# Down projection and second norm of a decoder layer: places of raw operands, order of their loads and splits, order of the norms' steps

## Chip, cores and metric

The kernel is one program on one core of one Trainium2 chip. The metric is the device time of one execution in microseconds (us). The engines named below are PE (TensorE, matrix products), DVE (VectorE), ACT (ScalarE), POOL (GpSimd) and SP (SyncE, whose queue issues most DMAs). PSUM is the memory in which PE accumulates; the kernel's PSUM tiles of 128 x 512 floats are called banks here.

## What is computed

One decoder layer in float32 on 1024 tokens of width 1024: two attention mixers, a gated merge, a norm, a SwiGLU feed-forward network of width 2816, and a second norm. The part that matters here is the last:

```python
def layer_norm(x, g, b):
    mu = jnp.mean(x, axis=-1, keepdims=True)
    xc = x - mu
    var = jnp.mean(xc * xc, axis=-1, keepdims=True)
    return xc * lax.rsqrt(var + LN_EPS) * g + b

def swiglu(u, w_gate_up, w_down):
    hg, hu = jnp.split(u @ w_gate_up, 2, axis=-1)
    return (silu(hg) * hu) @ w_down

y = mixer(x * (1.0 + scale_m) + shift_m, ...)
x = layer_norm(ALPHA * x + (1.0 + gate_m) * y, ln1_g, ln1_b)
y = swiglu(x * (1.0 + scale_f) + shift_f, ...)
x = layer_norm(ALPHA * x + (1.0 + gate_f) * y, ln2_g, ln2_b)
```

## The kernel before

**Two-term floats.** A float32 operand is held as two fp32r tiles, a rounded high part and the rest. `split` (L168) makes them: ACT copies the operand into the high tile (L169), then DVE subtracts that from the operand into the low tile (L170). A product of two operands is three matmuls (high x high, high x low, low x high; L1706).

**Seven products.** The down projection h (1024 tokens x 2816) times w_down (2816 x 1024) is done by Strassen's scheme in the Winograd form: seven products of half-size blocks in place of eight, over sums and differences of blocks. `ORDER` (L1521) gives their order, (0, 1, 2, 3, 5, 4, 6); the text counts them first to seventh as they are run. Each product has 11 units (NP), so the units are numbered u = 0 to 76. Unit u brings 128 rows of each operand, one tile from h and one from w_down, together 128 x 1024 floats, and makes 12 matmuls: four blocks of tokens (t), three terms each.

The sums of blocks (names `hs_d` and `wt2_d` in the code; the trace calls the second `wt_d`) are made earlier, during the up projection and the first products, by three "lanes" of `sum_set`, each with tiles of its own: it fetches four tiles, subtracts and adds on DVE, and writes four tiles to DRAM. `sums_ahead` (L1574) starts a lane's next set when the step p of the up projection is below a limit of that lane. The very last set, ("h", 10), is fetched on POOL's queue and not on ACT's.

**Loads and splits.** `dn_load` fetches a unit's two tiles on SP's queue (L1595, L1597) into a raw place: tiles `r1` and `r2` in two buffers each, so four places in turn. `dn_prepare` splits units up to a given one and, after each split, loads up to `ahead` = 4 units more. The split goes to an operand place (`dn_place`): eight tiles of pool `bigu`, six of `low`, two made of the small tiles `w_hi` and `w_lo` (these units are split in two halves of 512), and from unit 33 on one more, `a_raw` and `a_lo`. In the product loop `dn_prepare` stands at the start of unit u and runs 12, then 14, then 15 units ahead of PE.

**Banks and adds.** There are two sets of four banks. `bank_a` is used by the first, third, sixth and seventh product, `bank` by the second, and then again by the fourth and fifth. Three products start from zero (first, second, fourth in this order); every other one accumulates on top of what its banks hold, since in this scheme the results are running sums. After each product `dn_add` reads the banks: it multiplies by the gate (L1700) and adds to the tile `z` of the residual (L1701). The first matmul of the next product on that bank comes behind this read. The last three units of the fourth and fifth product (`shared`) are done block by block, so that a block is finished, and added, before the next one starts; the others before the seventh finish their four blocks in the last unit. The seventh is done block by block altogether: all 11 units for t = 0, then for t = 1, and so on.

**Norms.** `gain` (L1372, L1373) multiplies half a row block of `z` by the first norm's scale and adds its shift; there are 16 such pairs, placed by the table `GAINS` at (product, unit). `half_stats` (L1268) takes the moments of half a row block. `norm_shared` is a generator with three parts: moments and square root (L1273 to L1276); reciprocal, a small product and ACT's scaling of the row block (L1295 to L1297); scale, shift and the store (L1299 to L1301). `norm_steps` moves every norm in the list `norms` one part on. In the seventh product three rounds of `norm_steps` stand ahead of each block's add, and a fourth after it. The last block goes through `norm_quick`.

Instructions stand in program order on each engine (`manual_schedule`), so a `split` or a `gain` that stands ahead of a `dn_add` on DVE is done ahead of it.

## Time and profile before

| what | value |
|---|---|
| time, median of 3 runs | 1798.02 us (1797.59 to 1798.94) |
| the profiled execution's own time | 1797.99 us |
| span of its trace | 1796.2 us |
| PE busy | 1762.3 us, 98% |
| DVE busy | 1197.9 us, 67% |
| ACT busy | 846.0 us, 47% |
| POOL busy | 504.9 us, 28% |
| down projection, first to last matmul | 1554.03 to 1782.47 us |

The shares are means over the whole span, over stages with different limits; a single stage is read from the timeline and from the busy time in windows. In a timeline a row gives start, length, engine, line, operation, output<-inputs, tile shapes and a count of like instructions; in brackets stands the idle time ahead of it and who ended that. "Granted clock" is the share of its full speed that PE ran at. In a list of waits a row gives who waited for whom, the time in us, how many times, and the longest. `dn` names raw tiles and split operands alike, `pf` and `px` are banks, `zt` is the residual `z`, `g` the product of bank and gate.

### The profile page before, as it was taken

To read this page: it belongs to the slowest core of one execution; us is meant where nothing else is said; L and a number is where in the kernel's file an instruction comes from. 1 tells how busy PE (TensorE), PEld (TensorE's weight loads), DVE (VectorE), ACT (ScalarE), POOL (GpSimd) and SP (SyncE) were. 2 spreads that over 40 slices of the span, in tenths; PEclk is the share of its full clock that TensorE was granted. 3 is DMA by queue.
4 is the path that set the end of the run, shared out by engine and by line. 5 is a ranking of instruction groups with operands and counts; after the bars stand their busy time and mean duration, and the time that the engine had idled before them with its cause. 6 is when DMAs were issued, how large, how long until landed. Compare 5 with 4: busy or idle time off the path is not lost.

```text
span 1796.2 us, 24740 instructions
## 1 busy us (share of the span) xinstructions
PE 1762.3 (98%) x8774; PEld 1448.2 (81%) x8774; DVE 1197.9 (67%) x2141; ACT 846.0 (47%) x1739; POOL 504.9 (28%) x338
## 2 busy tenths in 40 slices
PE   9999999999999999999999999999999999999796
PEld 7888888888888888788888888888888888888585
DVE  7655566567566766658656865766666666578967
ACT  6554454544444677764441224743434333444431
POOL 0232233233233332125204753143334334100000
PEclk9999999999999999999999999999999999999898
DMA  9222323333332332266576442146656665587741
GB/s 363 84 69 80 104 78 91 109 90 94 97 89 83 85 101 72 71 241 226 174 239 222 162 132 100 36 164 226 229 214 244 212 245 189 196 273 234 244 143 71
DMA packets 130844, 277.30 MB, mean 154 GB/s; under 512 B 19296, under 2 KB 29088, under 8 KB 130720
## 3 DMA queue, kind: packets, MB, share of 16 engines
q1 hardware_dynamic: 116544, 246.80, 41.3%
q10 hardware_dynamic: 13392, 26.29, 4.4%
q0 software_dynamic: 784, 2.63, 0.4%
q8 instruction: 69, 1.13, 0.2%
q14 instruction: 55, 0.45, 0.1%
HBM read 203.99 MB, written 58.03 MB: 146 GB/s over the span
## 4 chain that ended last, share of the span: by engine, by line
PE 84%; DVE 10%; ACT 2%; DMA 2%; issue 1%; SPq 0%; DVEq 0%; ACTq 0%
PE pf L1037 21%; PE pj L191 9%; PE pj L193 9%; PE pj L192 9%; PE p L1037 6%; PE s L623 4%; PE p L191 3%; PE p L193 3%; PE p L192 3%; PE po L684 3%; PE pt L661 3%; PE pf L1706 2%; DVE dn L170 2%; DVE g L1700 1%; DVE zt L1701 1%
## 5 line engine op out<-in xcount | busy, mean ns | idle before, releaser
L191 PE MATMUL pj<-u,w_hi 128*128 128x512 f32 x736 | 302.7, 411 | 0.0
L193 PE MATMUL pj<-u,w_lo 128*128 128x512 f32 x736 | 288.8, 392 | 0.0
L192 PE MATMUL pj<-u,w_hi 128*128 128x512 f32 x736 | 288.2, 392 | 0.0
L550 POOL TENSOR_TENSOR rb<-rb,sin_t 128x512 f32<-128x512 f32 x64 | 85.7, 1339 | 518.2 <-DVE rb L548 483.4
L145 DVE TENSOR_TENSOR w_lo<-r,w_hi 128x512 fp32r<-128x512 f32 x128 | 122.7, 964 | 102.3 <-ACT w_hi L144 94.9
L79 DVE TENSOR_TENSOR w_lo<-w_raw,w_hi 128x512 fp32r<-128x512 f32 x132 | 122.9, 934 | 82.0 <-ACT w_hi L78 81.5
L191 PEld LDWEIGHTS pj<-u,w_hi 128*128 128x128 f32 x736 | 138.6, 188 | 31.6 <-issue 6.2
L1706 PE MATMUL pf<-dn 128*128 128x512 f32 x630 | 151.9, 395 | 11.5 <-DVE g L1700 11.5
L193 PEld LDWEIGHTS pj<-u,w_lo 128*128 128x128 f32 x736 | 138.3, 188 | 30.6
L639 ACT ACTIVATE probs<-probs,st 128x128 f32<-128x128 f32 (+1 forms) x320 | 145.6, 461 | 31.0 <-DVE st L628 30.7
L192 PEld LDWEIGHTS pj<-u,w_hi 128*128 128x128 f32 x736 | 138.9, 189 | 22.2
L1706 PEld LDWEIGHTS pf<-dn 128*128 128x128 f32 x630 | 119.6, 190 | 37.9 <-ACT dn L169 9.6
L78 ACT ACTIVATE w_hi<-w_raw 128x512 fp32r<-128x512 f32 x132 | 81.8, 622 | 93.1 <-PE p L192 55.0
L551 POOL TENSOR_TENSOR r<-ra,rb 128x512 f32<-128x512 f32 x63 | 116.1, 1843 | 4.9
L663 ACT ACTIVATE ptsb<-pt 128x512 f32<-128x512 f32 (+1 forms) x128 | 63.5, 548 | 101.5 <-PE pt L661 101.2
L169 ACT ACTIVATE dn<-dn 128x1024 fp32r<-128x1024 f32 x66 | 69.6, 1059 | 84.6 <-DMA dn<-wt_d 35.1
L170 DVE TENSOR_TENSOR dn<-dn 128x1024 fp32r<-128x1024 f32 x66 | 79.1, 1221 | 40.2 <-ACT dn L169 40.0
L564 ACT ACTIVATE qs<-r 64x1024 fp32r<-64x1024 f32 x38 | 40.2, 1058 | 100.1 <-POOL r L551 99.6
L144 ACT ACTIVATE w_hi<-r 128x512 fp32r<-128x512 f32 x128 | 79.4, 622 | 12.5 <-DVE gate L1499 4.9
L126 POOL TENSOR_TENSOR s<-r 128x512 f32<-128x512 f32 x27 | 35.8, 1327 | 174.9 <-DVE w_lo L145 92.1
L565 DVE TENSOR_TENSOR qs<-r,qs 64x1024 fp32r<-64x1024 f32 x38 | 46.4, 1220 | 57.2 <-ACT qs L564 56.5
L623 PE MATMUL s<-kh,qs 128*128 128x256 f32 (+1 forms) x320 | 79.7, 283 | 1.8 <-DVE st L628 1.7
(447 smaller groups left out, 4321.5 us busy)
## 6 DMA issues: line engine op xcount, KB each, us to landing
w_raw<-in_w_in SPq DMA_DIRECT2D x100, 256.0 KB
r<-in_w_gate_up SPq DMA_DIRECT2D x44, 512.0 KB
a_raw<-in_w_ada SPq DMA_DIRECT2D x24, 512.0 KB
dn<-hs_d SPq DMA_DIRECT2D x44, 256.0 KB
dn<-wt_d SPq DMA_DIRECT2D x44, 256.0 KB
h_d<-g SPq DMA_DIRECT2D x39, 256.0 KB
dn<-h_d SPq DMA_DIRECT2D x33, 256.0 KB
dn<-in_w_down SPq DMA_DIRECT2D x33, 256.0 KB
```

Of the source, the lines that this page charges most:

```text
L79: self.nc.vector.tensor_tensor(lo, raw, hi, op=OP.subtract)
L145: self.nc.vector.tensor_tensor(lo, src, hi, op=OP.subtract)
L170: nc.vector.tensor_tensor(lo, src, hi, op=OP.subtract)
L191: nc.tensor.matmul(ps, w[0], m[0], start=first, stop=False)
L192: nc.tensor.matmul(ps, w[0], m[1], start=False, stop=False)
L193: nc.tensor.matmul(ps, w[1], m[0], start=False, stop=last)
L550: eng.tensor_tensor(b, b, sin_t[:, s], op=OP.mult)
L551: eng.tensor_tensor(residue_half(res, r, t), by_residue(a, r), by_residue(b, r), op=OP.add)
L623: nc.tensor.matmul(pss[h][:, i, lo:], box["q"][h][:, b * P:(b + 1) * P], ks[h][:, (b - 1 + lo) * P:(b + 1) * P], start=i == 0 and n == 0, ...
L639: nc.scalar.activation(pr, pr, AF.Exp, scale=-1.0, bias=st[:, 0, h, b:b + 1], accum_out=st[:, 1, h, b:b + 1])
L1037: nc.tensor.matmul(ps, w[:, c], m[:, k], start=first and k == 0 and n == 0, stop=k == 3 and n == 2, skip_group_check=True)
L1706: nc.tensor.matmul(ps, op[x][0][:, c], op[y][1], start=first and n == 0, stop=last and n == 2, skip_group_check=True)
```

## The change

**Raw places.** A function `raw_place` gives them now. Units 0 to 11 use the same four. From unit 12 on the two small operand places become raw places, four of them (two in the tiles of `w_hi` and two in those of `w_lo`, under the name `dnw`), eight in all, and from unit 36 on `a_raw` and `a_lo` make it ten. The operand places are the fourteen of `bigu` and `low` alone. Units whose raw tiles are small ones are split in two halves of 512, the others whole.

**Distance.** In the product loop `dn_prepare` runs 13 units ahead of PE throughout, and loads run nine units ahead of the split, where it was four.

**Scale and shift.** `GAINS` places four pairs in each of the first four products; it was four, two, four, two and four in the first five.

**Last sums.** The first lane may start a set one step of the up projection later (p < 21, where it was 20), which leaves the lane of `a_raw` and `a_lo` free for the last set.

**Norms.** The norm of block 3 joins the list after the first add of the sixth product, and not after its last. In the seventh product rounds of `norm_steps` stand only ahead of the first and the last block's add; after a block's add its own norm does its first two parts at once, and then one round moves the norms that stand in the list already.

```diff
for lane, first in enumerate(((4, 0), (8, 0), (4, 3))):
             if lanes[lane] and next(lanes[lane], "end") == "end":
                 lanes[lane] = None
-            if (not lanes[lane] and (p, i) > first and p < (20, NF + 1, 19)[lane] and sets
+            if (not lanes[lane] and (p, i) > first and p < (21, NF + 1, 19)[lane] and sets
                     and (sets[0][0] == "w" or 2 * sets[0][1] + 1 < p - (p < NF and i < 3))):
                 lanes[lane] = sum_set(*sets.pop(0), *lane_tiles(lane))
                 next(lanes[lane])
 
-    dn_raw, dn_op = {}, {}
+    dn_raw, dn_op, loaded = {}, {}, [0]
     DN = 7 * NP
 
+    raw_places = ["r2", "r1"] * 2
+
+    def raw_place(u):
+        if u == 12:
+            raw_places[:0] = ["w_hi", "w_lo"] * 2
+        if u == 36:
+            raw_places[:0] = ["a_raw", "a_lo"]
+        place = raw_places.pop(0)
+        raw_places.append(place)
+        if place[0] == "w":
+            return [wpool.tile([P, 512], F32, name="dnw", tag=place, bufs=4) for _ in range(2)]
+        pool, bufs = (gx, 2) if place[0] == "r" else (ev, 1)
+        raw = pool.tile([P, 2, TH], F32, name="dn", tag=place, bufs=bufs)
+        return [raw[:, 0], raw[:, 1], raw]
+
     def dn_load(upto):
-        while len(dn_raw) < min(upto, DN):
-            u = len(dn_raw)
+        while loaded[0] < min(upto, DN):
+            u = loaded[0]
+            loaded[0] += 1
             i, j = ORDER[u // NP], u % NP
-            raw = gx.tile([P, 2, TH], F32, name="dn", tag="r1" if u % 2 else "r2", bufs=2)
-            dn_raw[u] = raw
+            raw = dn_raw[u] = raw_place(u)
             f = 2 * j + (i in (1, 5, 6))
             rows = slice(f * P, (f + 1) * P)
-            nc.sync.dma_start(raw[:, 0], {0: h_d[f][:, H0], 1: h_d[f][:, H0], 2: hs_d[j, 0], 3: hs_d[j, 3], 4: hs_d[j, 1],
+            nc.sync.dma_start(raw[0], {0: h_d[f][:, H0], 1: h_d[f][:, H0], 2: hs_d[j, 0], 3: hs_d[j, 3], 4: hs_d[j, 1],
                                           5: hs_d[j, 2], 6: h_d[f][:, H1]}[i])
-            nc.sync.dma_start(raw[:, 1], {0: I["w_down"][rows, H0], 1: I["w_down"][rows, H0], 2: wt2_d[j, 3], 3: wt2_d[j, 0],
+            nc.sync.dma_start(raw[1], {0: I["w_down"][rows, H0], 1: I["w_down"][rows, H0], 2: wt2_d[j, 3], 3: wt2_d[j, 0],
                                           4: wt2_d[j, 1], 5: I["w_down"][rows, H1], 6: wt2_d[j, 2]}[i])
-
-    places = ["bigu"] * 8 + ["low"] * 6 + ["w"] * 2
-
-    def dn_place(u):
-        if u == 33:
-            places.insert(0, "a")
-        place = places.pop(0)
-        places.append(place)
-        if place == "w":
-            hi, lo = [[wpool.tile([P, 512], F32R, name=s, tag=s, bufs=4) for _ in range(2)] for s in ("w_hi", "w_lo")]
-            for i in range(2):
-                split(hi[i], lo[i], dn_raw[u][:, i])
-            return hi, lo
-        if place == "a":
-            hl = [ev.tile([P, 2, TH], F32R, name=n, tag=n, bufs=1) for n in ("a_raw", "a_lo")]
-        else:
-            op = pools[place].tile([P, 2, 2, TH], F32R, name="dn", tag="big")
-            hl = [op[:, x] for x in range(2)]
-        split(*hl, dn_raw[u])
-        return [[x[:, i] for i in range(2)] for x in hl]
 
     def dn_prepare(upto, ahead):
         while len(dn_op) < min(upto, DN):
             u = len(dn_op)
             dn_load(u + 1)
-            dn_op[u] = dn_place(u)
+            op = dn_op[u] = pools["bigu" if u % 14 < 8 else "low"].tile([P, 2, 2, TH], F32R, name="dn", tag="big")
+            raw = dn_raw.pop(u)
+            if len(raw) == 3:
+                split(op[:, 0], op[:, 1], raw[2])
+            else:
+                for i in range(2):
+                    split(op[:, 0, i], op[:, 1, i], raw[i])
             dn_load(u + 1 + ahead)
 
     n = 0
...
             if p > 1:
                 next(ada, None)
     gb1 = norm_params(1)
-    GAINS = {(0, 3): (0, 0), (0, 5): (1, 0), (0, 7): (2, 0), (0, 9): (3, 0), (1, 5): (0, 1), (1, 7): (1, 1),
-             (2, 3): (2, 1), (2, 5): (3, 1), (2, 7): (4, 1), (2, 9): (5, 1), (3, 3): (6, 1), (3, 5): (7, 1),
-             (4, 2): (4, 0), (4, 4): (5, 0), (4, 6): (6, 0), (4, 8): (7, 0)}
+    GAINS = {(n, (2 if n == 3 else 3) + t * (1 if n == 3 else 2)): (t + n // 2 * 4, (n + 1) // 2 % 2) for n in range(4) for t in range(4)}
 
     def dn_add(tb, eh, ps, first):
         es = slice(eh * 512, (eh + 1) * 512)
...
     def dn_mac(ps, u, t, first, last):
         op, c = dn_op[u], slice(t * P, (t + 1) * P)
         for n, (x, y) in enumerate(((0, 0), (0, 1), (1, 0))):
-            nc.tensor.matmul(ps, op[x][0][:, c], op[y][1], start=first and n == 0, stop=last and n == 2,
+            nc.tensor.matmul(ps, op[:, x, 0, c], op[:, y, 1], start=first and n == 0, stop=last and n == 2,
                              skip_group_check=True)
 
     st8 = gx.tile([P, TH], F32, name="s3", bufs=1)
...
         shared = NP - 3 if i in (3, 4) else NP
         for j in range(shared):
             u = n * NP + j
-            dn_prepare(u + (12 if u < 3 else 14 if u < 22 else 15), 4)
+            dn_prepare(u + 13, 9)
             for t in range(4):
                 dn_mac(ps[t], u, t, i in (0, 1, 3) and j == 0, j == NP - 1)
-            sums_ahead(NF, 1)
+            sums_ahead(NF, u)
             norm_steps()
             if (n, j) in GAINS:
                 gain(*GAINS[n, j], gb1)
...
             if not first:
                 half_stats(tb0 + t, eh)
             if shared < NP:
-                dn_prepare(n * NP + shared + 15 + t, 4)
+                dn_prepare(n * NP + 21 + min(t, 1), 9)
                 norm_steps()
-    norms.append(norm_shared(3, gb2, out))
+                if (i, t) == (4, 0):
+                    norms.append(norm_shared(3, gb2, out))
     for t in range(4):
         for j in range(NP):
             dn_mac(bank_a[t], 6 * NP + j, t, False, j == NP - 1)
-        for _ in range(3):
+        if t in (0, 3):
             norm_steps()
         dn_add(4 + t, 0, bank_a[t], True)
         half_stats(4 + t, 0)
         if t == 3:
             norm_quick(7, gb2, out)
         else:
-            norms.append(norm_shared(4 + t, gb2, out))
+            x = norm_shared(4 + t, gb2, out)
+            next(x)
+            next(x)
             norm_steps()
+            norms.append(x)
 
 
 def _chunks(w, kc):
```

Three places show how the instructions move.

The first is DVE from the splits of units 47 and 48 to the fourth product's first add, before (`dn<-dn` is a whole split, `w_lo` a half one, `a_lo` the split of unit 50, L1372 and L1373 a scale-and-shift pair, L1700 and L1701 the add):

```order
L170 TENSOR_TENSOR w_lo<-dn,w_hi 128x512 x4
L170 TENSOR_TENSOR dn<-dn 128x1024
L170 TENSOR_TENSOR a_lo<-dn,a_raw 128x1024
L1372 TENSOR_TENSOR zt<-zt,gb 128x512
L1373 TENSOR_TENSOR zt<-zt,gb 128x512
L170 TENSOR_TENSOR dn<-dn 128x1024 x2
L1372 TENSOR_TENSOR zt<-zt,gb 128x512
L1373 TENSOR_TENSOR zt<-zt,gb 128x512
L170 TENSOR_TENSOR dn<-dn 128x1024 x2
L1700 TENSOR_TENSOR g<-pf,gate_10913 128x512
L1701 SCALAR_TENSOR_TENSOR zt<-zt,g 128x512
L170 TENSOR_TENSOR dn<-dn 128x1024
```

The same engine and place after the change, from the split of unit 48 on (the add is L1699 there):

```order
L170 TENSOR_TENSOR dn<-dnw,dn 128x512 x2
L1372 TENSOR_TENSOR zt<-zt,gb 128x512
L1373 TENSOR_TENSOR zt<-zt,gb 128x512
L170 TENSOR_TENSOR dn<-dnw,dn 128x512 x2
L1372 TENSOR_TENSOR zt<-zt,gb 128x512
L1373 TENSOR_TENSOR zt<-zt,gb 128x512
L170 TENSOR_TENSOR dn<-dnw,dn 128x512 x2
L1372 TENSOR_TENSOR zt<-zt,gb 128x512
L1373 TENSOR_TENSOR zt<-zt,gb 128x512
L170 TENSOR_TENSOR dn<-dnw,dn 128x512 x2
L170 TENSOR_TENSOR dn<-dn 128x1024
L1699 TENSOR_TENSOR g<-pf,gate_10913 128x512
```

The last split ahead of the add is that of unit 52, where it was unit 54; four scale-and-shift pairs stand in the fourth product (three of them in these rows), where there were two; units 48 to 51 are split in halves.

The second is DVE in the seventh product, from the third block's add to the fourth's, before (L1268 to L1275 moments of the third block, L1295 and L1296 its reciprocal and small product, L1299 and L1300 a whole row block's scale and shift):

```order
L1700 TENSOR_TENSOR g<-pf,gate_10913 128x512
L1701 SCALAR_TENSOR_TENSOR zt<-zt,g 128x512
L1268 BN_STATS s_14060<-zt 128x6
L1273 BN_AGGR bmv<-s_14060 128x2
L1275 TENSOR_SCALAR brs<-bmv 128x1
L1295 RECIPROCAL brs<-brs 128x1
L1296 SCALAR_TENSOR_TENSOR brs<-bmv,brs 128x1
L1299 TENSOR_TENSOR zt<-zt,gb 128x1024
L1300 TENSOR_TENSOR zt<-zt,gb 128x1024
L1700 TENSOR_TENSOR g<-pf,gate_10913 128x512
```

And after (the add is L1699 and L1700 there):

```order
L1699 TENSOR_TENSOR g<-pf,gate_10913 128x512
L1700 SCALAR_TENSOR_TENSOR zt<-zt,g 128x512
L1268 BN_STATS s_14062<-zt 128x6
L1273 BN_AGGR bmv<-s_14062 128x2
L1275 TENSOR_SCALAR brs<-bmv 128x1
L1295 RECIPROCAL brs<-brs 128x1
L1296 SCALAR_TENSOR_TENSOR brs<-bmv,brs 128x1
L1299 TENSOR_TENSOR zt<-zt,gb 128x1024
L1300 TENSOR_TENSOR zt<-zt,gb 128x1024
L1299 TENSOR_TENSOR zt<-zt,gb 128x1024
L1300 TENSOR_TENSOR zt<-zt,gb 128x1024
L1699 TENSOR_TENSOR g<-pf,gate_10913 128x512
```

Before, one block's scale and shift stand between these two adds, and it is the third block's own. After, two blocks' stand there: first the second block's, whose scaling by ACT was asked for one block earlier, and then the third's.

The third is SP's queue from the load of unit 11 on, before, with the semaphores on which each DMA waits (a name and a running number; `DMAHW0` to `DMAHW7` count DMAs that have landed, `gb` are the first norm's scale and shift):

```order
L1595 DMA dn<-h_d 128x512 [waits DMAHW1_49,DVE_49]
L1597 DMA dn<-in_w_down 128x512 [waits DMAHW2_49]
L1260 DMA gb<-in_ln_g 128x1024 [waits DMAHW3_49]
L1260 DMA gb<-in_ln_b 128x1024 [waits DMAHW4_49]
L1595 DMA dn<-h_d 128x512 [waits DMAHW5_49,DVE_49]
```

And after:

```order
L1610 DMA dn<-h_d 128x512 [waits DMAHW1_49,DVE_49]
L1612 DMA dn<-in_w_down 128x512 [waits DMAHW2_49]
L1260 DMA gb<-in_ln_g 128x1024 [waits DMAHW3_49]
L1260 DMA gb<-in_ln_b 128x1024 [waits DMAHW4_49]
L1610 DMA dnw<-h_d 128x512 [waits DMAHW5_49,PE_49]
L1612 DMA dnw<-in_w_down 128x512 [waits DMAHW6_49,PE_49]
L1610 DMA dnw<-h_d 128x512 [waits DMAHW7_49]
```

Unit 12 goes to small tiles and waits for PE's last use of them; before it waited for DVE's split of a unit four ahead. The semaphores of the DMAs go round by eights in both.

## The prediction

> **What bounds the kernel now.** I read the page first, then busy time by stage, TensorE's (PE's) timeline, the waits of VectorE (DVE), ScalarE (ACT) and the load queue, and last DVE's timeline. The page gives the time in which everything below must lie:
>
> ```profile
> span 1796.2 us, 24740 instructions
> ```
>
> Busy time in the down projection, in stretches of 30 us (columns: stretch, length, busy time of PE, PEld, DVE, ACT and POOL, granted clock, DMA share, GB/s):
>
> ```profile
> 1614.00:1644.00 30.00, 30.00 (x134) 24.85 (x133) 23.24 (x30) 12.05 (x13) 0.00 (x0) 1.00 0.65 211
> 1644.00:1674.00 30.00, 29.94 (x132) 24.41 (x130) 27.73 (x34) 13.49 (x15) 0.00 (x0) 1.00 0.71 234
> 1674.00:1704.00 30.00, 18.44 (x60) 13.49 (x61) 26.63 (x32) 14.40 (x15) 0.00 (x0) 0.72 0.81 268
> ```
>
> PE fills the first two and is the bound there; a faster helper engine would bring nothing. The third loses 11.6 us of PE and a quarter of its clock. PE's timeline there and at the ends of the stage (start, length, count of matmuls; in brackets the idle time before and who ended it):
>
> ```profile
> 1554.03 31.44 PE L1706 MATMUL pf<-dn 128*128 128x512 f32 x138
> ...
> 1669.70 4.24 PE L1706 MATMUL px<-dn 128*128 128x512 f32 x18
> 1683.17 1.62 PE L1706 MATMUL pf<-dn 128*128 128x512 f32 x3 [9.23 <-DVE g L1700]
> 1685.54 1.65 PE L1706 MATMUL pf<-dn 128*128 128x512 f32 x3 [0.76 <-DVE g L1700]
> 1688.01 1.65 PE L1706 MATMUL px<-dn 128*128 128x512 f32 x3 [0.82 <-DVE g L1700]
> 1690.47 1.65 PE L1706 MATMUL px<-dn 128*128 128x512 f32 x3 [0.81 <-DVE g L1700]
> 1691.91 2.76 PE L1706 MATMUL pf<-dn 128*128 128x512 f32 x6
> ...
> 1720.60 22.60 PE L1706 MATMUL pf<-dn 128*128 128x512 f32 x99
> ...
> 1752.17 0.93 PE L1706 MATMUL pf<-dn 128*128 128x512 f32 x3 [1.48 <-DVE g L1700]
> ...
> 1776.17 6.30 PE L1706 MATMUL pf<-dn 128*128 128x512 f32 x27
> ```
>
> The first row gives the pace: a matmul of 0.39 us starts every (31.44 - 0.39) / 137 = 0.2266 us, so a unit's twelve take 2.72. The stage's 924 need 209.4 us; from 1554.03 to 1782.47 they took 228.4. No row waits for an operand. What ends every wait is DVE's add, L1700, which reads a bank on top of which the next product accumulates: 11.6 us are lost ahead of the fifth product, which begins at 1683.17, and then three matmuls last 1.65, where three at full pace last 0.93 or less; 1.48 are lost ahead of the seventh. After PE's end at 1782.47 there are 13.7 us of norms and stores.
>
> Why is DVE late with this add? Its waits from its first work on unit 12 to the fourth product's first add (1574.6 to 1682.3), and in the same stretch ACT's two largest and the load queue's largest (who waited for whom, us, times, longest):
>
> ```profile
> DVE dn L170 <- ACT dn L169: 18.2, 11, 3.7
> DVE w_lo L170 <- ACT w_hi L169: 1.2, 1, 1.2
> DVE a_lo L170 <- DMA dn<-hs_d: 0.5, 1, 0.5
> ```
>
> ```profile
> ACT dn L169 <- DMA dn<-wt_d: 27.1, 16, 7.9
> ACT dn L169 <- DMA dn<-in_w_down: 17.7, 12, 3.4
> ```
>
> ```profile
> SPq L1595 <- DVE dn L170: 48.5, 31, 8.4
> ```
>
> This is a ring. DVE's half of a split waits for ACT's half, ACT's for a load, and the load for one of four raw places, which DVE's half sets free. DVE stood 19.9 us in it, and its adds stand in order behind the splits of units that PE needs only much later.
>
> **The change, part by part.** What a piece of DVE's work costs where it runs without a pause:
>
> ```profile
> 1614.29 4.62 DVE L170 TENSOR_TENSOR dn<-dn 128x1024 fp32r<-128x1024 f32 x4
> 1618.83 0.69 DVE L1372 TENSOR_TENSOR zt<-zt,gb 128x512 f32<-128x512 f32 x1
> 1619.55 0.69 DVE L1373 TENSOR_TENSOR zt<-zt,gb 128x512 f32<-128x512 f32 x1
> 1620.16 1.28 DVE L170 TENSOR_TENSOR w_lo<-dn,w_hi 128x512 fp32r<-128x512 f32 x2
> ```
>
> ```profile
> 1682.34 0.69 DVE L1700 TENSOR_TENSOR g<-pf,gate 128x512 f32<-128x512 f32 x1
> 1683.06 0.69 DVE L1701 SCALAR_TENSOR_TENSOR zt<-zt,g 128x512 f32<-128x512 f32 x1
> 1683.67 1.22 DVE L170 TENSOR_TENSOR dn<-dn 128x1024 fp32r<-128x1024 f32 x1
> ```
>
> By the starts, a split takes 4.54 / 4 = 1.135, a scale-and-shift pair 1.33 and an add 1.33. A split in two halves lasts 1.28 from first start to last end, where a whole one lasts 1.22: 0.06 more.
>
> *Raw places, loads, scale and shift.* DVE's time at the fourth product's first add was 1682.34. Without the 19.9 of waits it is 1662.4. All sixteen scale-and-shift pairs now stand ahead of this add, and twelve did: 4 x 1.33 = 5.3 more. Of the units 12 to 52, twenty are split in halves, six were: 14 x 0.06 = 0.8. Units 53 and 54 no longer stand ahead of it: 2 x 1.135 = 2.3 less. That makes 1666.2, if no wait is left. The loads that hide behind DVE's work are then asked for eight to ten splits ahead, over 9 us of DVE's time alone. If that cover fails, the waits come back one for one.
>
> Some stay in any case. Loads 0 to 11 still have four places, and the longest early wait, 3.1, is for unit 12's load, which stands behind load 11 on its queue as before. The waits ahead of 1600, and the DMA engines at that time:
>
> ```profile
> DVE dn L170 <- ACT dn L169: 9.8, 6, 3.1
> ```
>
> ```profile
> 1560.00:1600.00 40.00, 40.00 (x178) 33.15 (x177) 27.90 (x32) 18.25 (x20) 2.21 (x4) 1.00 0.90 308
> ```
>
> At a share of 0.90 the engines could carry little more, so between 0 and 9.8 us of waits remain. I take 4, the 3.1 and a little, for the queue is no longer held back after it: 1670.2.
>
> How late may it be? Without a stop PE asks for the fourth bank of the fifth product at 1554.03 + 44 x 2.72 + 3 x 0.68 = 1675.8. From its first add DVE has three adds, two splits and the last bank's read ahead of that: 4.0 + 2.3 + 0.7 = 7.0, so it must begin by 1668.8. At 1670.2 PE stands 1.4 us. The sixth product then begins at 1554.03 + 55 x 2.72 + 1.4 = 1705.0 and not at 1720.60: **15.6 gained**, of it 11.6 - 1.4 = 10.2 of standing and 5.4 of slow clock.
>
> For the clock I take nothing after a stand of 1.4: after the 1.48 three matmuls lasted 0.93, full pace, and only after 9.23 were they slow. The Trainium skill (TensorE: Matmul & The Clock Gate, What's actually happening) has the clock halved after an idle window of about 3.4 us; both stands agree with that. It leaves the forecast alone and bears on the first rival.
>
> *Operand places and queues.* Fourteen operand places in place of sixteen, later seventeen, hold splits at most 12 units, 33 us, ahead of PE. DVE's lateness of 20 us at the first adds is below that, so no matmul waits for an operand. The new wait of the load queue for PE, at the first w places, has all later loads and two stores of sums behind it; PE's last work on these tiles ends by 1554, before the queue gets there, so it costs nothing. The second norm's scale and shift are fetched behind loads nine ahead, still 20 us before use: nothing.
>
> *Sixth product.* DVE adds the fifth as PE leaves it and then goes through the norms' chain with ACT, up to the sixth's first add. These starts are that first fifth add, the first sixth add and the last add of all:
>
> ```profile
> 1718.76 0.69 DVE L1700 TENSOR_TENSOR g<-pf,gate 128x512 f32<-128x512 f32 x1 [3.80 <-PE pf L1706]
> ...
> 1751.34 0.68 DVE L1700 TENSOR_TENSOR g<-pf,gate 128x512 f32<-128x512 f32 x1
> ...
> 1787.62 0.68 DVE L1700 TENSOR_TENSOR g<-pf,gate 128x512 f32<-128x512 f32 x1
> ```
>
> The chain keeps its order. Two of its splits are in halves, and DVE can start when ACT has done the first; the gain is bounded by 0 and by PE's 1.48. I take **0.8**.
>
> *Tail.* From the add at 1751.34 to the one at 1787.62 DVE took 36.3 us, with this wait in it:
>
> ```profile
> DVE zt L1299 <- ACT zt L1297: 5.2, 4, 1.3
> ```
>
> Afterwards the same instructions stand between these two adds, but each tile's products come one block later, after ACT's scaling is done, so the 5.2 go. Units 75 and 76 are split behind the first and second add and not before: 2 x 1.135, and some 0.2 of waiting for ACT. 36.3 - 5.2 + 2.5 = 33.6: **2.7 gained**. PE, released 0.8 after the first add, needs 132 x 0.2266 = 29.9 to its end, so the last add waits for DVE and not for PE.
>
> Sum: the profiled execution took 1797.99, its span and 1.8 outside it; the median of the runs shown is 1798.02. Less 15.6, 0.8 and 2.7: **1778.9**.
>
> **The rivals.** *DVE stays late.* All 9.8 of early waits remain: the add comes at 1676.0 and PE stands 7.2, 5.8 more than forecast: 1784.7. With the slow clock that followed 9.23, up to 5.4 more: 1790.1. By the skill's window it would be the upper end. For it speaks the DMA share of 0.90; against, that loads to come need no longer wait for a place.
>
> *The places are not what holds loads back.* The queue's DMAs use eight semaphores in turn, so that four units are in flight at most, as before. If all 19.9 stay, the add comes at 1686.1, 3.8 later than it did, and sixth product and tail give back 3.5: 1798.3, no change. Against it: 48.5 us of the queue's waits are for DVE.
>
> *Slower.* Bandwidth is short, not places. The last sum's two rows of h, 1 MB, can now be fetched beside loads 8 to 15, about 20 us sooner, and the waits of DVE grow, at the same bank and one for one. From 23.2 us of waits (add at 1689.4) the time is 0.2% up; at 25 it is 1803.4. Against it: 211 and 234 GB/s from 1614 to 1674, where 308 was reached before.
>
> *The tail brings nothing*, ACT or the stores being late: 1781.6.
>
> **How the numbers follow.** Forecast 0.63, DVE late 0.24, no effect 0.05, slower 0.05, tail nothing 0.03. About 0.2%, 3.6 us, is what a measurement of this kernel can tell from no change. Faster: 0.63 + 0.24 + 0.03 = 0.90; same 0.05; slower 0.05. The range goes from no stand at all and 1 us more in the sixth product and tail (1776.5) to the middle of the first rival (1787.4), which leaves out about 0.1 for its upper half and 0.1 for the rest.
>
> **What would show it.** Right: PE waits under 3 us for the add ahead of the fifth product, at a clock of 1.00; the sixth product begins near 1705; DVE waits some 4 us for ACT in that stretch, all before 1600; the last add starts within 3 us of PE's end. Wrong: ACT still waits for loads after 1600, DVE reaches that add after 1673, or a matmul waits for an operand.

## The result and the profile after

The changed kernel took **1781.41 us** (median of six runs, 1779.73 to 1785.0), the kernel before 1797.80 (1796.91 to 1801.46). The ratio is 0.9907, 95% interval 0.9894 to 0.992: 16.4 us faster, where 19.1 was forecast (1778.9).

The profile after is that of the run of 1785.0, the longest of the six. Its span, and its busy time in the stretches shown for before:

```profile
span 1783.2 us, 24796 instructions
```

```profile
1614.00:1644.00 30.00, 30.00 (x134) 24.86 (x133) 29.55 (x42) 15.27 (x19) 0.00 (x0) 1.00 0.74 251
1644.00:1674.00 30.00, 30.00 (x134) 24.82 (x133) 29.62 (x44) 10.99 (x14) 0.00 (x0) 1.00 0.76 258
1674.00:1704.00 30.00, 27.93 (x114) 22.03 (x113) 20.68 (x25) 11.15 (x15) 0.00 (x0) 0.94 0.68 228
```

DVE, 23.24 and 27.73 busy in the first two stretches before, is now all but full in both (29.55 and 29.62). The third loses 2.1 us of PE and 0.06 of its clock, where it lost 11.6 and 0.28. PE's timeline at the joints of the products:

```profile
1557.44 31.45 PE L1705 MATMUL pf<-dn 128*128 128x512 f32 x138
...
1678.18 0.96 PE L1705 MATMUL pf<-dn 128*128 128x512 f32 x3 [0.21 <-DVE g L1699]
1680.64 0.97 PE L1705 MATMUL px<-dn 128*128 128x512 f32 x3 [1.50 <-DVE g L1699]
1681.97 1.19 PE L1705 MATMUL px<-dn 128*128 128x512 f32 x3 [0.36 <-DVE g L1699]
1682.96 2.76 PE L1705 MATMUL pf<-dn 128*128 128x512 f32 x6
...
1711.57 30.08 PE L1705 MATMUL pf<-dn 128*128 128x512 f32 x132
1742.49 7.31 PE L1705 MATMUL pf<-dn 128*128 128x512 f32 x31 [0.84 <-DVE g L1699]
1750.86 23.23 PE L1705 MATMUL pf<-dn 128*128 128x512 f32 x101 [1.06 <-DVE dn L170]
```

The first row shows something that has nothing to do with the change: the down projection began at 1557.44, 3.4 later than in the profile before. In the 13 other profiles of this study its start lies between 1553.86 and 1556.85, and a second profile of the same kernel began at 1554.32. So all stages are compared below from their own first matmul. The fifth product now loses 2.07 of standing, in three pieces, and after them six matmuls take 2.76 where 1.52 is full pace. The last row is a wait that the prediction said would not be: PE waits for the split of a unit.

DVE's waits and the load queue's largest in the stretch shown for before (1574.6 to 1682.3), and the splits of units 10 and 11 and of unit 12 in DVE's timeline:

```profile
DVE dn L170 <- ACT dn L169: 7.5, 2, 4.5
```

```profile
SPq L1610 <- DVE dn L170: 39.9, 32, 8.4
```

```profile
1578.49 2.36 DVE L170 TENSOR_TENSOR dn<-dn 128x1024 fp32r<-128x1024 f32 x2 [4.52 <-ACT dn L169]
1583.79 1.31 DVE L170 TENSOR_TENSOR dn<-dnw,dn 128x512 fp32r<-128x512 f32 x2 [2.94 <-ACT dn L169]
```

Two waits are left, both in the first 27 us of the stage. The 4.52 is for unit 10, whose wait in the kernel before lay just ahead of the stretch shown:

```profile
1571.99 2.58 DVE L170 TENSOR_TENSOR dn<-dn 128x1024 fp32r<-128x1024 f32 x2 [1.94 <-ACT dn L169]
```

So like for like 2.94 is left of 19.9 from unit 12 on. After unit 12 DVE waits for nothing until its adds are done: the ring no longer holds it up. The load queue still waits 39.9 for DVE's splits, 48.5 before; with ten places between them DVE doesn't wait for that.

The table has all the profiles but the two with work on POOL, in us from the first matmul of the down projection: the start of the fourth product's first add, the standing of PE for adds ahead of the fifth product, the starts of the sixth and seventh, DVE's last add, and the end of the span.

| kernel | 4th's first add | stand | 6th | 7th | last add | end | median of its runs, ratio to before (95%) |
|---|---|---|---|---|---|---|---|
| before | 128.31 | 11.62 | 166.57 | 198.14 | 233.59 | 242.17 | 1797.80 |
| forecast | 116.2 | 1.4 | 151.0 | 181.7 | 214.5 | 223.1 | 1778.9 |
| changed | 117.54 | 2.07 | 154.13 | 185.05 | 217.18 | 225.76 | 1781.41, 0.9907 (0.9894 to 0.992) |
| changed, again | 116.18 | 0.99 | 151.18 | 182.10 | 214.17 | 222.78 | 1778.86, one run |
| before, new norms | 127.83 | 11.13 | 165.91 | 197.48 | 228.29 | 236.92 | 1794.18, 0.9979 (0.997 to 0.9988) |
| before, new table | 128.34 | 11.65 | 166.77 | 198.34 | 233.80 | 242.36 | 1801.11, 1.0018 (1.001 to 1.0027) |
| the same, again | 130.31 | 13.59 | 168.08 | 199.65 | 235.11 | 243.69 | 1800.64, one run |
| changed, old table and norms | 113.76 | 0 | 149.60 | 180.53 | 218.56 | 227.14 | 1784.30, 0.9924 (0.9912 to 0.9936) |
| changed, old table | 113.76 | 0 | 149.60 | 180.54 | 212.65 | 221.28 | 1778.75, 0.9891 (0.9878 to 0.9904) |
| changed, four places | 122.42 | 5.66 | 158.54 | 193.13 | 225.44 | 234.05 | 1792.68, 0.9969 (0.9957 to 0.9981) |
| changed, four ahead | 115.16 | 0.25 | 150.16 | 181.07 | 213.16 | 221.73 | 1781.31, 0.9905 (0.989 to 0.992) |
| changed, four ahead, old limit | 117.39 | 1.86 | 154.00 | 184.92 | 216.99 | 225.64 | 1780.46, 0.9905 (0.989 to 0.992) |
| changed, adds first | 115.75 | 0 | 149.60 | 180.51 | 212.58 | 221.16 | 1778.53, 0.9884 (0.987 to 0.9899) |

The first profile of the changed kernel has a stage 16.4 shorter than before, as much as the medians differ; that the two agree is partly chance, since the second profile gives 19.4. Of the 6.1 between these two runs, 3.1 lie ahead of the stage and 3.0 in it.

### The profile page after: what moved, and what is told of

It reads as the page before. It is cut to its first block, busy times and chain, and to the rows that moved or that the text cites. A ratio compares the mean times of both kernels' runs of the same rounds, so it can differ in the third digit from the quotient of the medians.

```text
span 1783.2 us, 24796 instructions
## 1 busy us (share of the span) xinstructions
PE 1761.1 (99%) x8774; PEld 1446.9 (81%) x8774; DVE 1199.7 (67%) x2161; ACT 847.7 (48%) x1759; POOL 506.6 (28%) x338
## 4 chain that ended last, share of the span: by engine, by line
PE 82%; DVE 9%; DMA 4%; ACT 2%; issue 2%; POOL 0%; SPq 0%; DVEq 0%; ACTq 0%
PE pf L1037 21%; PE pj L191 9%; PE pj L193 9%; PE pj L192 9%; PE p L1037 5%; PE s L623 4%; PE p L191 3%; PE p L193 3%; PE p L192 3%; PE po L684 3%; PE pt L661 3%; PE pf L1705 2%; DVE dn L170 2%; DVE qs L565 1%; PE px L1705 1%
## 5 line engine op out<-in xcount | busy, mean ns | idle before, releaser
L1705 PE MATMUL pf<-dn 128*128 128x512 f32 x726 | 171.9, 392 | 2.1 <-DVE dn L170 1.1
L1705 PEld LDWEIGHTS pf<-dn 128*128 128x128 f32 x726 | 136.9, 189 | 31.8 <-DVE dn L170 1.5
L551 POOL TENSOR_TENSOR r<-ra,rb 128x512 f32<-128x512 f32 x63 | 116.2, 1845 | 4.9
L623 PE MATMUL s<-kl,qs 128*128 128x256 f32 (+1 forms) x320 | 80.1, 280 | 0.0
L169 ACT ACTIVATE dn<-dn 128x1024 fp32r<-128x1024 f32 x49 | 51.5, 1060 | 52.7 <-PE px L1705 17.2
```

What stands on the lines that cost most here:

```text
L551: eng.tensor_tensor(residue_half(res, r, t), by_residue(a, r), by_residue(b, r), op=OP.add)
L623: nc.tensor.matmul(pss[h][:, i, lo:], box["q"][h][:, b * P:(b + 1) * P], ks[h][:, (b - 1 + lo) * P:(b + 1) * P], start=i == 0 and n == 0, ...
L1705: nc.tensor.matmul(ps, op[:, x, 0, c], op[:, y, 1], start=first and n == 0, stop=last and n == 2, skip_group_check=True)
```

## Experiments

The theory: four raw places held the loads back, DVE stood in the ring behind them, and its adds came late; ten places end that. Rivals: the distance of nine units does it, or the splits at 13 units, or the norms' order; and the places do nothing since four units are in flight at most anyway. The splits at 13 units and the fourteen operand places were not run by themselves.

### The changed kernel once more

No edit.

> The changed kernel once more, as it is, for a second profile. Theory (the early waits, 7.5 us in its first profile and 3.4 to 5.7 in the kernels with the same early part, differ from run to run; its median stands for less than its first profile shows): between 20 us after the start of the down projection and the fourth product's first add DVE waits 3.5 to 6, the add is at 115 to 117, PE stands under 2 ahead of the fifth product, and the stage takes 221.7 to 225 us where it took 225.8. Rival (7.5 belongs to this kernel): add at 117.5, stage 225.8.

Its DVE waits in the same stretch, its splits, the fourth product's first add, and PE around its stands:

```profile
DVE dn L170 <- ACT dn L169: 3.7, 1, 3.7
```

```profile
1573.21 2.36 DVE L170 TENSOR_TENSOR dn<-dn 128x1024 fp32r<-128x1024 f32 x2 [2.65 <-ACT dn L169]
1579.25 3.41 DVE L170 TENSOR_TENSOR dn<-dnw,dn 128x512 fp32r<-128x512 f32 x5 [3.67 <-ACT dn L169]
...
1670.50 0.68 DVE L1699 TENSOR_TENSOR g<-pf,gate 128x512 f32<-128x512 f32 x1
```

```profile
1554.32 31.44 PE L1705 MATMUL pf<-dn 128*128 128x512 f32 x138
...
1676.16 0.96 PE L1705 MATMUL px<-dn 128*128 128x512 f32 x3 [0.63 <-DVE g L1699]
1677.48 0.96 PE L1705 MATMUL px<-dn 128*128 128x512 f32 x3 [0.36 <-DVE g L1699]
1678.28 1.54 PE L1705 MATMUL pf<-dn 128*128 128x512 f32 x6
...
1705.50 30.08 PE L1705 MATMUL pf<-dn 128*128 128x512 f32 x132
```

The add is at 1670.50 - 1554.32 = 116.18, and the sixth product begins at 151.18. The theory holds: the early waits differ from run to run. What differs is when the loads of units 10 and 11 land: ACT's half of unit 10's split waits 5.91 for its load in the first profile and 3.14 here. The splits of the two units begin 21.05 after the start in the first profile, 18.89 here, 17.96 before, and 17.1 to 19.9 in all others.

### Four raw places

```diff
-        if u == 12:
+        if u == 1200:
...
-        if u == 36:
+        if u == 3600:
```

> The changed kernel with the four old raw places for all units; loads nine ahead, splits 13 ahead, fourteen operand places, new table and norms stay. Theory (the places make the ring): DVE waits some 15 us or more ahead of the fourth product's first add, which comes 126 to 129 us after the start of the down projection, PE stands about 9 ahead of the fifth product, and only the 0.65 of the sixth and the 3.3 of the tail are left of the gain: 1793 to 1795. Rival (distance, or splits at 13 units ahead in place of 15, make the gain): 1781 to 1784.

DVE's waits from 1574.6 to 1682.3, PE's stands, and two waits of DVE during the sixth product (1715 to 1750):

```profile
DVE dn L170 <- ACT dn L169: 13.0, 8, 4.4
```

```profile
1680.10 0.93 PE L1705 MATMUL pf<-dn 128*128 128x512 f32 x3 [3.41 <-DVE g L1699]
1682.47 1.65 PE L1705 MATMUL pf<-dn 128*128 128x512 f32 x3 [1.44 <-DVE g L1699]
...
1749.98 31.78 PE L1705 MATMUL pf<-dn 128*128 128x512 f32 x132 [4.51 <-DVE g L1699]
```

```profile
DVE zt L1299 <- DMA gb<-in_ln_g: 2.1, 1, 2.1
DVE zt L1300 <- DMA gb<-in_ln_b: 0.9, 1, 0.9
```

1792.68: 11.3 of the 16.4 go with the places. The time came 0.3 below what was written, but not all by the way that was written: the first add came at 122.4 and not at 126 or later, DVE waited 13.0 and not 15, and a stand of 4.51 appeared ahead of the seventh product. That stand goes with the second norm's scale and shift. SP asks for them 172.0 after the stage's start, where it was 146.7 with ten places, and DVE waits 3.0 for them in the chain ahead of the sixth's add. That they stand behind loads which wait for a place, nine ahead, is argued from SP's order; no run had four places and loads four ahead.

So the 11.3 are not all the ring. From the start of the sixth product to that of the seventh it takes 34.59, where the changed kernel takes 30.92: 3.7 come from that stand, 3.0 of it DVE's wait for scale and shift. At the start of the sixth product this kernel is 4.4 and 7.4 behind the two profiles of the changed kernel. And there it is still 8.0 ahead of the kernel before, with the same four places. In part this is plain: units 53 and 54 no longer stand ahead of the add (2.3). But from unit 12 on DVE also waits only 10.7, where it was 19.9. Four more pairs stand in those waits; with the new table alone (below) 15.6 and 16.6 were left, so some 5 to 6 less are the doing of other parts of the change, and it stays open of which.

### Loads four ahead, and the old limit of the lane

```diff
-            dn_prepare(u + 13, 9)
+            dn_prepare(u + 13, 4)
...
-                dn_prepare(n * NP + 21 + min(t, 1), 9)
+                dn_prepare(n * NP + 21 + min(t, 1), 4)
```

> The changed kernel with loads four units ahead of the split and not nine; its ten places stay. Theory (a load leaves when its place is free; the distance only sets where the stores of the last two sums stand among the loads in SP's order): the fourth product's first add comes 0 to 3 us later than in the changed kernel, 117.5 to 120.5 us from the start of the down projection: 1781 to 1785. Rival (the distance hides the loads): the waits of the kernel before after its first 45 us, 10 us, come back, the add is at 127 and the time is over 1790.

The stand ahead of the fifth product in its timeline:

```profile
1677.02 0.96 PE L1705 MATMUL px<-dn 128*128 128x512 f32 x3 [0.25 <-DVE g L1699]
```

1781.31, the same as with nine (1781.41). With ten places the distance makes no difference: a load's place in the code orders it among SP's other DMAs, and it leaves when its place is free.

On top of this, the lane's limit was put back to `p < 20`:

> The changed kernel with loads four units ahead and with the old limit of the first lane (p < 20), so that the last sum's rows of h are fetched later; to be compared with the changed kernel at four units ahead. Theory (the earlier fetch of 1 MB takes DMA time from the loads of units 8 to 15, when the DMA engines are full): unit 12's split starts 2 to 3 us sooner after the start of the down projection than 26.35, and the time is 2 to 4 us less than that of the kernel at four ahead. Rival A (the engines are full either way): the same. Rival B (the last sum's stores now hold up the loads behind them in SP's order): 3 us or more slower, with DVE waiting after 40 us.

The splits of unit 12 on, first at four ahead and then with the old limit as well:

```profile
1578.80 5.38 DVE L170 TENSOR_TENSOR dn<-dnw,dn 128x512 fp32r<-128x512 f32 x8 [3.39 <-ACT dn L169]
```

```profile
1579.22 5.28 DVE L170 TENSOR_TENSOR dn<-dnw,dn 128x512 fp32r<-128x512 f32 x8 [3.37 <-ACT dn L169]
```

They start 23.93 and 23.76 after the stage's start, with the same wait, and the medians agree: rival A. The old limit's profile has a stage 3.9 longer, by 2.3 of waits for later splits; with one profile of each it stays open whether SP's order or the run makes these. In the changed kernel the DMA engines are at a share of 0.96 and 0.99 from 1560 to 1600 (its two profiles) where 0.90 was before, and still the last sum's earlier fetch costs nothing that shows. The later limit brings nothing that shows, either.

### The new table alone, and the old table in the changed kernel

The edit is the lines of `GAINS` in the change, put into the kernel before.

> The kernel before with the new table of scale-and-shift pairs alone. Theory (DVE's work ahead of the fourth product's first add counts one for one): four pairs of 1.33 more stand there, the add and the fifth product come 5.3 later: 1803.1. Rival A (the loads pace DVE, so work put into its waits is free): two pairs fall in the second product, where DVE still waits 6.5 us, and are hidden; two fall in the fourth, where 1.7 of waits are left: 1798.7 to 1800.5. Rival B (all hidden): 1797.8.

PE's stand ahead of the fifth product in the first profile, and in a second:

```profile
1684.91 1.62 PE L1704 MATMUL pf<-dn 128*128 128x512 f32 x3 [9.26 <-DVE g L1698]
```

> The kernel before with the new table once more, for a second profile: its median stood 3.5 above before's, while in its first profile the fourth product's first add came 128.34 after the start of the down projection, as in before (128.31), and the stage took 242.4 (before 242.2). Theory (the four pairs lie in DVE's waits): add at 127.5 to 129, stage 241.5 to 243. Rival (the first profile was a lucky run, and two or more pairs count): add at 130 or later, stage 244 or more.

```profile
1686.24 1.62 PE L1704 MATMUL pf<-dn 128*128 128x512 f32 x3 [11.22 <-DVE g L1698]
```

The add came 0.0 and 2.0 later than before, not 5.3: in the ring most of DVE's added work goes into its waits. So the theory of one for one fell here. In the second profile the add, at 130.31, lies in the range of the rival that two or more pairs count, and the stage, 243.69, just short of it. The median says 3.5 slower, and its interval (1.001 to 1.0027) is clear of no change. The stage shows 0.2 and 1.5 of this; the first profile is of the second shortest of eleven runs, and where the rest arises isn't settled.

Now the changed kernel with the old table, and with the old norms' order as well (the tail of the kernel before, with the two splits at their new places):

> The changed kernel with the old table of scale-and-shift pairs. Theory (the four pairs moved ahead of the fourth product's first add cost what is left there): the 2.07 of standing and the 2.4 of slow clock ahead of the fifth product go: 1781.4 - 4.5 = 1776.9. Rival A (the four pairs that return to the fifth product make DVE late for the fifth's adds or the sixth's norms): 1779 to 1783. Rival B (the stand had another cause): 1781.4.

> The changed kernel with the old table of scale-and-shift pairs and the old order of the norms' steps, so raw places, loads, splits and last sums alone. Theory (the raw places make the gain of the fifth product): DVE's add is 4 x 1.33 = 5.3 ahead of the changed kernel's, no stand is left ahead of the fifth product, 17.0 gained there and 0.65 in the sixth; the old tail has units 75 and 76 to split as well, 2.3 later: 1797.8 - 17.0 - 0.65 + 2.3 = 1782.5. Rival (without the new table the places bring less, DVE still comes late): over 1787, with more than 3 us of standing ahead of the fifth product.

In the first, PE's rows behind the fifth product, and one of DVE's waits:

```profile
1706.22 30.08 PE L1707 MATMUL pf<-dn 128*128 128x512 f32 x132
1737.16 7.29 PE L1707 MATMUL pf<-dn 128*128 128x512 f32 x31 [0.86 <-DVE g L1701]
1745.53 23.21 PE L1707 MATMUL pf<-dn 128*128 128x512 f32 x101 [1.08 <-DVE dn L170]
```

```profile
DVE g L1701 <- PE pf L1707: 3.1, 1, 3.1
```

Here DVE is 3.1 early at the fourth product's add and waits for PE; no stand is left, and the sixth product begins at 149.60, which is 55 units of 2.72. Without that wait the add would stand at 113.76 - 3.1 = 110.7. In the kernel "adds first" below, with the new table and the same early waits (splits of units 10 and 11 at 18.1, then 3.95), it stands at 115.75: 5.1 later. So outside the ring the four pairs count nearly one for one. Both medians came 1.8 above what was written. The old table is 2.7 better in the medians; the intervals overlap, so the size rests on the profiles: 4.5 against the first, 1.5 against the second.

### The norms' order alone

The edit is the last hunk of the change, with `dn_prepare` left as it was.

> The kernel before with the new order of the norms' steps alone. Theory (the new order pays in the tail whatever else is done): PE's end stays where it is, still with about 9 us of standing ahead of the fifth product, but the last add comes right behind PE's end, 1787.62 - 1782.5 = 5.1 earlier: 1797.8 - 5.1 = 1792.7. Rival A (the sum's net figure, which charged two splits to the tail, holds here too): 1795.1. Rival B (stores or ACT bound the tail, or its gain came only from DVE being less late): 1797.8.

PE's rows at the start and the end of the seventh product, and DVE's last add:

```profile
1752.96 0.93 PE L1706 MATMUL pf<-dn 128*128 128x512 f32 x3 [1.49 <-DVE g L1700]
...
1776.97 6.29 PE L1706 MATMUL pf<-dn 128*128 128x512 f32 x27
```

```profile
1783.77 0.68 DVE L1700 TENSOR_TENSOR g<-pf,gate 128x512 f32<-128x512 f32 x1
```

From the seventh product's start to the end it is 1792.4 - 1752.96 = 39.4, where it was 44.0: 4.6 by the order alone, with the last add 0.5 behind PE's end at 1783.26. The median gives 3.4, between theory and rival A. Set beside the kernel with old table and old norms, whose stage is 5.9 longer than with the new, it shows that the tail's gain doesn't hang on the rest.

### The adds ahead of the splits

```diff
-                dn_prepare(n * NP + 21 + min(t, 1), 9)
+                dn_prepare(n * NP + (21 + min(t, 1) if i == 4 else 20), 9)
```

> The changed kernel with units 53 and 54 split behind the fourth product's four adds and not between them. Theory (the two splits in between, 2.3 us, and not only the first add's time, set the stand, and the slow clock follows from the sum of the stands within some 4 us): with the first add at 117.5 the last bank is read by 122.2, where PE wants it at 121.7: a stand of 0.5, no slow clock, the sixth product at 150.1 from the start: 1.5 of standing and 2.4 of slow clock less than in the first profile of the changed kernel, 1777.5, and 1 less where DVE is not late anyway. Rival A (any stand costs the clock): 1779. Rival B (the splits put off make PE wait for an operand in the fifth product): 1781.4 or more, with a wait for a split.

PE's rows ahead of the fifth product and on:

```profile
1669.54 4.24 PE L1705 MATMUL px<-dn 128*128 128x512 f32 x18
1673.62 1.52 PE L1705 MATMUL pf<-dn 128*128 128x512 f32 x6
1674.98 1.52 PE L1705 MATMUL px<-dn 128*128 128x512 f32 x6
```

No stand, with the first add at 115.75. In the changed kernel as it is, an add at 116.18 left 0.99. The prediction's limit of 1668.8 (114.8 from the start) moves by the two splits, 2.3, to 117.1, and 115.75 lies below it. No matmul of the fifth product waits for a split, so rival B falls. The median, 1778.53, lies between the theory's 1777.5 and rival A's 1779. Since there was no stand at all, what a short stand does to the clock wasn't tested by this, and the interval (0.987 to 0.9899) overlaps that of the changed kernel.

### What bounds the tail

PE's wait of 1.06 for unit 76 was taken away by splitting it one block sooner, and, to relieve DVE, the scale and shift of one row block went to POOL (old table in both):

```diff
-                dn_prepare(n * NP + 21 + min(t, 1), 9)
+                dn_prepare(n * NP + (22 if i == 4 else 21 + min(t, 1)), 9)
...
-        nc.vector.tensor_tensor(z, z, gb[:, 0], op=OP.mult)
-        nc.vector.tensor_tensor(z, z, gb[:, 1], op=OP.add)
+        eng = nc.gpsimd if tb == 4 else nc.vector
+        eng.tensor_tensor(z, z, gb[:, 0], op=OP.mult)
+        eng.tensor_tensor(z, z, gb[:, 1], op=OP.add)
```

> The changed kernel with the old table, with unit 76 split behind the sixth product's first add and not its second, and with the scale and shift of row block 4 on POOL in place of DVE. Theory (after the old table DVE's own work and the 1.08 wait for unit 76 bound the tail): no wait for an operand in the seventh product; DVE has 2 x 1.22 less up to the last add, which then comes right behind PE's end, 1.5 us sooner: 1.5 below the changed kernel with the old table. Rival (POOL's two steps slow DVE's beside them, or the block's store comes late): no gain, or 1 us slower.

1778.96 (0.9897, 0.988 to 0.9913), against 1778.75 without these edits. PE ended 1.4 sooner in the stage (210.7), the last add only 0.2 (212.4). POOL's two steps, and DVE's beside them:

```profile
1755.74 2.40 POOL L1300 TENSOR_TENSOR zt<-zt,gb 128x1024 f32<-128x1024 f32 x1 [184.22 <-ACT zt L1297]
1758.22 2.42 POOL L1301 TENSOR_TENSOR zt<-zt,gb 128x1024 f32<-128x1024 f32 x1
```

```profile
1757.39 0.77 DVE L1296 SCALAR_TENSOR_TENSOR brs<-bmv,brs 128x1 f32<-128x1 f32 x1
...
1759.32 1.86 DVE L1703 SCALAR_TENSOR_TENSOR zt<-zt,g 128x512 f32<-128x512 f32 x1
```

With block 5 in place of block 4 on POOL, and the same DVE step:

> The changed kernel with the old table, unit 76 split behind the sixth product's first add, and the scale and shift of row block 5, not 4, on POOL. In the run with block 4 on POOL the last add came no sooner, since between the last two adds DVE still had two blocks to scale and shift, 4.9 us, and a DVE step of 0.69 beside POOL's took 1.86. Theory (2.45 less between the last two adds): the last add comes right behind PE's end, 211.0 to 211.5 from the start of the down projection, and the stage takes 219.5 to 220 where the changed kernel with the old table took 221.3. Rival (POOL's steps, 4.9 long, hold up the DVE steps beside them by 1 to 2 us again, or the block's store ends last): 221 or more.

```profile
1761.07 2.18 DVE L1703 SCALAR_TENSOR_TENSOR zt<-zt,g 128x512 f32<-128x512 f32 x1
```

1778.73 (0.9884, 0.9867 to 0.9902), stage 222.1: the rival in both. With block 4 on POOL, 2.45 was taken from DVE up to the last add: 1.8 came back in the two longer steps, 0.44 as a wait for PE, and 0.2 was gained. With block 5 the two products were taken out between the last two adds themselves, and the last add came 0.8 later than without any of this.

## Why the prediction was right, and where it was short

**Right: the ring and its end.** With four places 11.3 of 16.4 are gone; with loads four ahead nothing is. Of the 11.3, 3.7 belong to the stand ahead of the seventh product, most of it for the late scale and shift, so for the ring itself 4.4 to 7.4 are shown, at the start of the sixth product. The sum let all of the waits end by the places; the run with four of them has only 10.7 of 19.9 left, so other parts of the change shorten them too, which the prediction didn't see. The rival that loads are held by what may be in flight is refuted by the places. The slower rival is refuted by the time, and the lane's old limit, with loads four ahead, changed nothing that shows. One sentence of the step was beside the point: that loads are asked for eight to ten splits ahead. The cover is the ten places; with them the number nine does nothing.

**Right: the limit and the pace.** The sum had the add at 116.2 and a stand of 1.4; the second profile has 116.18 and 0.99, and the sixth product at 151.18 where 151.0 was forecast. That this profile fits so well is partly luck: the first has 117.54, 2.07 and 154.13.

**Short: the early waits.** "I take 4, the 3.1 and a little" was made from unit 12 on, and there 2.9 and 3.7 came. It left out that the loads of units 10 and 11 can land later than in the one profile at hand. In the first profile they did, by 3.1 against the kernel before, and the add came 1.4 late. This is the rival "DVE stays late" in part, in one of two profiles. That the median lies 2.5 above the forecast fits a mixture of the two, but the other runs have no profile.

**Short: the clock.** "I take nothing after a stand of 1.4" held at 0.99 in two pieces. At 2.07 in three it did not: the sixth product began at 154.13 and not at 149.6 + 2.07, so 2.5 went to slow clock and stretched matmuls. One microsecond of it, with the granted clock of 0.50 as the third number from the end:

```profile
1683.00:1684.00 1.00, 1.00 (x4) 0.81 (x3) 1.00 (x2) 0.80 (x2) 0.00 (x0) 0.50 0.00 0
```

**Missed: a wait for an operand.** "No matmul waits for an operand" was worked out for the places and forgot unit 76, which is now split behind the second add of the sixth product while PE needs it at the end of the seventh's first block. It waited 1.06 and 1.05 in the two profiles of the changed kernel. It cost little, since DVE ends the tail: without it, and with block 4's products on POOL, the last add moved 0.2.

**Tail and sixth product.** Forecast 2.7 and 0.8; from the seventh's start to the end 44.03 became 40.71 and 40.68, 3.3 less, and from the sixth's start to the seventh's 31.57 became 30.92 in both, 0.65 less. The waits of DVE between the sixth's first add and the last, 6.5 in all, fell to these:

```profile
DVE brs L1295 <- ACT brs L1276: 1.0, 3, 0.3
DVE dn L170 <- ACT dn L169: 0.2, 1, 0.2
```

The 5.2 went as forecast. The tail gained 0.6 more than that sum gave: 0.3 of it is a wait that the sum didn't count, which fell from 1.3 to 1.0, and the rest isn't traced.

**The signs.** Of the signs of being wrong that the prediction named, all three were seen in the first profile, though the gain came. After 1600 ACT still waits for loads, 11.6 in the first profile (36.4 before), but DVE doesn't wait for ACT there:

```profile
ACT dn L169 <- DMA dn<-wt_d: 6.1, 8, 1.7
ACT dn L169 <- DMA dnw<-hs_d: 5.5, 3, 2.6
```

DVE reached the add at 1674.98, past 1673, but only because the stage began 3.4 late. And a matmul waited for an operand, unit 76's. A sign of being right failed there as well: the clock was not 1.00 behind the stand.

**The table of pairs.** Four pairs at 5.3 was nearly right for the changed kernel (5.1). In the kernel before they don't count one for one: the add moves by 0.0 and 2.0. Without this part the change does no worse and perhaps better: 1778.75, with an interval that overlaps, and a stage 4.5 and 1.5 shorter than in the two profiles.

## What to carry to other kernels

Where a load waits for a buffer that the stalled engine itself sets free, count the buffers, not the distance in the code. Work added to an engine inside such a ring may move its later steps by less than its own length, and once the ring is gone it counts almost in full, so a reordering that looked cheap has to be priced again. When a part of a change is taken out, ask what the parts left in do without it: part of what the four places cost here was a new wait. One profile is one run: before a small wait is put into a sum, look at what its landing times did in another profile of the same code.

## What the runs showed of the hardware

PE's clock fell to half after stands that were each short: 0.21, 1.50 and 0.36 within 4.0 us (1677.97 to 1681.97). With four ahead and the old limit 1.50 and 0.36 did it as well:

```profile
1678.52 0.97 PE L1705 MATMUL px<-dn 128*128 128x512 f32 x3 [1.50 <-DVE g L1699]
1679.85 1.63 PE L1705 MATMUL px<-dn 128*128 128x512 f32 x3 [0.36 <-DVE g L1699]
```

Three matmuls of 1.63 are at half pace. A single stand of 1.48, and 0.63 with 0.36, left it at full speed. The Trainium skill (TensorE: Matmul & The Clock Gate, What's actually happening) puts the fall after an idle window of about 3.4 us. In these two profiles no stand ahead of the fall was longer than 1.5, so it doesn't take one gap of that length; how much standing within what time is enough isn't shown.

Beside POOL's steps, 2.4 us long with block 4 and 3.29 and 2.73 with block 5, a DVE step of 0.69 took 1.86 and 2.18. One of 0.16 took 0.77 and ended at 1758.16, where POOL's step ended at 1758.14. The Trainium skill (SBUF — State Buffer, SBUF: two separate sides) says that DVE's steps with two operands from SBUF and POOL's share a port pair that one holds for its whole step; the trace agrees with that.
